# Row sums of the gates and the shift on VectorE, filler tiles at other places of the stream

## The chip, the cores and the metric

The kernel runs on one core of a Trainium2 chip. The metric is the device time of one execution in microseconds. Five engines work side by side, each through its own list of instructions in order: TensorE (PE in the profile; PEld is its weight load), VectorE (DVE), ScalarE (ACT), GpSimd (POOL) and SyncE (SP), which here only issues transfers. An instruction that waits holds up everything behind it on its engine.

## The reference

One step of a hybrid backbone with one layer: 128 context tokens and 512 latent tokens, 640 in all, of width 2048. Cut to what matters:

```
mod = silu(c) @ w_mod + b_mod            # for latent and for context: two vectors of 3 * 2048
shift, scale, gate = split(mod, 3)
h = rms_norm(x, norm_w) * (1 + scale) + shift
proj = h @ w_in                          # u_f, z_f (512 each), q, k, v, z_d (1536 each), a/b (48)
y_f = fft(u_f).real * silu(z_f)
q, k, v = silu(short_conv(q, k, v))      # q and k normalised
o = gated_delta_scan(q, k, v, a, b)      # 12 heads of 128, forward and backward
y = concat(y_f, rms_norm(o) * silu(z_d)) @ w_out
out = rms_norm(x + gate * y)
```

The gate needs `silu(c) @ w_mod[:, 4096:6144]` for two vectors; the shift's part in `u_f` needs `shift @ w_in[:, 0:512]`. Both are sums of 2048 weight rows, each row weighted by one number for each of the two vectors. These are the row sums of this case.

## The kernel before, in words

**Stages.** To about 200 us the kernel normalises the tokens, forms scale and shift and starts the projection. Then comes the stream: 53 tiles of 128 columns of `w_in` (`stream`, L1341), each 96 matmuls at L1354: 16 blocks of 128 rows, two halves of 320 tokens, three products of high and low parts of weight and token. ACT loads the weights (`raw`) and rounds them (`whi`, L1330), POOL subtracts (`wlo`, L1338). After the stream comes the output projection (L1622).

**Heads.** Between the stream's matmuls stand the short steps of the twelve heads, each a generator: `conv` (L731), `blocks` (L811), `solve` (L868), `decay` (L951), `prep` (L1002), `scan` (L1055), `head_out` (L1146). In `solve`, DVE builds small inverses, SP stores them to DRAM (`xd`) and loads them back in eight transfers, four `DD` (L912) and four `DP` (L915); DVE transposes `DD` (L918) and PE multiplies (L929, L940). A scan walks five blocks from both ends: PE gives keys and queries times state (L1072, L1079), DVE forms `r` (L1075), PE (L1091) and ACT (L1094) make `vn`, PE makes the update (L1099) from which DVE forms the new state `S` (L1106), and the output (L1111), which DVE adds (L1118, L1121). At its end come squares on ACT (L1137), a sum on DVE (L1139), a power on POOL (L1141) and a scaling on DVE (L1143); then `head_out` transposes the output on PE (L1154).

**Order.** All of it is recorded in one program order by a builder. `Estimate` (L72) keeps a clock for each engine with assumed costs. A generator yields the engine its next step needs and the time from which it may be recorded; `advance` (L1413) records every step that is due before the stream goes on. Ranks (L1656) decide between steps: scans and solves have low numbers, `res_gates` has 10, the last. The order that results is fixed; the real engines then wait wherever the assumed times were too short.

**Order of the tiles.** `names` (L1300) starts with u0 to u3, k1, q1, v1, z0, z1, f0, f1, f2; then each head h from 2 brings k, v, q and a filler, z of the head before (none for head 2; z10, f3, z11 for head 11). A tile k or q of head i may be handed over only when head i-2's scan is done, v only when the one before has been read (`needs`, L1480); until then the stream stalls.

**The row sums.** `rows256` (L1265) sums 256 columns: four loads of 512 KB into one buffer `gw`, after each four 32-wide matmuls that lie side by side in PE (L1273), and one addition into `ga` on DVE (L1276; L1278 the first time). It is called twice for the shift (`shift_u`, L1253) and eight times for the gates (`res_gates`, L1282). For the shift, PE then sums the four partition groups and turns them (L1260). For the gates it sums them (L1291), DVE adds the bias (L1292), which SP has loaded (L1288), and SP stores two rows (L1294). The Fourier steps wait for all gates to be done.

Of the kernel before, what the change touches and what calls it, by code (L numbers as in the profile page):

```python
# [9 lines left out]
F32 = mybir.dt.float32  # L10
F32R = mybir.dt.float32r
AF = mybir.ActivationFunctionType
ALU = mybir.AluOpType
# [4 lines left out]
P = 128  # L18
DM = 2048
NK = DM // P  # L20
# [51 lines left out]
class Estimate:  # L72
# [107 lines left out]
    def __call__(self, inst, *_):  # L180
        outs = [x.bass_ap for x in inst.outs if getattr(x, "bass_ap", None) is not None]
        ins = [x.bass_ap for x in inst.ins if getattr(x, "bass_ap", None) is not None]
        if not outs:
            return
        engine = str(inst.engine).split(".")[-1]
        if engine not in self.free:
            return
        op = str(inst.opcode)
        by = "DMA" if "DMA" in op else engine
        t = max([self.free[engine]] + [self.after(x, by, False) for x in ins] + [self.after(x, by, True) for x in outs])  # L190
        if by == "DMA":
            self.free[engine] = t + 0.06
            size = 4
            for _, count in outs[0].ap:
                size *= count
            piece = max(4, min(self.run(outs[0]), self.run(ins[0]), 8192))
            begin = max(t + 1.4, self.dma)
            self.dma = begin + size / piece * (7 + 0.043 * piece) / 16e3
            end = self.dma + 0.7
        else:  # L200
            end = t + self.cost(op, engine, inst, outs, ins)
            self.free[engine] = end
            if engine == "PE":
                end += 0.2
        for x in ins:
            self.note(x, end, by, False)
        for x in outs:
            self.note(x, end, by, True)
        self.last = max(self.last, end)
# [3 lines left out]
def hybrid_step(ctx: ExitStack, tc: tile.TileContext, x_prompt, x_sample, state_ctx, c, c_ctx,  # L213
# [3 lines left out]
    PE, ACT, DVE, POOL, SP = nc.tensor, nc.scalar, nc.vector, nc.gpsimd, nc.sync  # L217
    est = Estimate()
# [10 lines left out]
    def bank():  # L229
        return ps_g.tile([P, 512], F32, tag="g", name="bank")  # L230
# [6 lines left out]
    def K(name):  # L237
        a, b = CST[name]
        return cst[:, a:b]
# [4 lines left out]
    gates_d = dram.tile([2, DM], F32, name="gates_d")  # L244
# [23 lines left out]
    csh = const.tile([P, NK, 32], F32, name="csh")  # L268
# [282 lines left out]
    g = Pools()  # L551
# [316 lines left out]
    def solve(h):  # L868
# [42 lines left out]
        for b in range(4):  # L911
# [1 line left out]
                         in_=xd[10 * b:10 * b + 10].rearrange("u r c -> r u c"))  # L913
            o = 32 * (b ^ 1)
            SP.dma_start(out=DP[o:o + 32], in_=xd[10 * b + 5:10 * b + 10].rearrange("u r c -> r u c"))  # L915
        yield "V"
        f2, N = "p d t c -> p (d t c)", s["N"]
        DVE.transpose(DD[:, 2:4].rearrange(f2), DD[:, 0:2].rearrange(f2))  # L918
        yield
# [330 lines left out]
        yield  # L1250


    def shift_u():  # L1253
        while "ebias" not in done:
            yield "poll"
        for i in range(2):
            ga = yield from rows256(win_v[:, :, 256 * i:256 * i + 256], csh)
            pg = bank()
            for q in range(2):
                PE.matmul(pg[:, 2 * q:2 * q + 2], lhsT=ga[:, P * q:P * (q + 1)], rhs=K("sel_mod"), start=True, stop=True)  # L1260
            DVE.tensor_copy(ubias[:, 2 * i:2 * i + 2].rearrange("p i m -> p (i m)"), pg[:, 0:4])
            yield
        done.add("ubias")

    def rows256(src, lhs):  # L1265
        ga = g.tile([P, 256], F32, tag="ga", name="ga", bufs=1)
        for j in range(4):
            gw = g.tile([P, 4, 256], F32, tag="gw", name="gw", bufs=1)
            SP.dma_start(out=gw, in_=src[:, 4 * j:4 * j + 4])
            yield "P", est.last + 3.0  # L1270
            pg = bank()
            for q in range(4):
                PE.matmul(pg[32 * q:32 * q + 32, 0:256], lhsT=lhs[:, 4 * j + q, :], rhs=gw[:, q, :], start=True, stop=True,  # L1273
                          tile_position=(0, 32 * q))
            if j:
                DVE.tensor_tensor(ga, ga, pg[:, 0:256], ALU.add)  # L1276
            else:
                DVE.tensor_copy(ga, pg[:, 0:256])  # L1278
        yield
        return ga  # L1280

    def res_gates():  # L1282
        yield from shift_u()
        for i in range(8):
            ns = slice(2 * DM + 256 * i, 2 * DM + 256 * i + 256)
            ga = yield from rows256(wmv[:, :, ns], cz)
            bt = g.tile([P, 4, 256], F32, tag="gw", name="gbt", bufs=1)[0:2, 0]
            SP.dma_start(out=bt, in_=b_mod[0, ns].partition_broadcast(2))  # L1288
            yield "P", est.last + 1.0
            pg = bank()  # L1290
            PE.matmul(pg[0:2, 0:256], lhsT=K("sel_mod"), rhs=ga, start=True, stop=True)  # L1291
            DVE.tensor_tensor(bt, bt, pg[0:2, 0:256], ALU.add)  # L1292
            yield "S"
            SP.dma_start(out=gates_d[:, 256 * i:256 * i + 256], in_=bt)  # L1294
            yield
        done.add("res_gates")


    place = {"k": C_K, "v": C_V, "q": C_Q, "z": C_ZD, "u": 0, "f": 512}
    names = "u0 u1 u2 u3 k1 q1 v1 z0 z1 f0 f1 f2".split()  # L1300
    fill = {2: "", 11: "z10 f3 z11"}
    for h in range(2, NH):
        names += [f"k{h}", f"v{h}", f"q{h}"] + fill.get(h, f"z{h - 1}").split()
    tiles = [(n[0], int(n[1:]), place[n[0]] + P * int(n[1:])) for n in names]
# [396 lines left out]
```

## Time and profile before

| | us |
|---|---|
| median of three runs (lowest, highest) | 1458.52 (1456.28, 1462.25) |
| the profiled execution, own time | 1462.74 |
| its span in the trace | 1460.9 |
| PE busy, of the span | 1400.6 |
| DVE, ACT, POOL busy | 695.1, 670.8, 627.6 |

The span runs from the first to the last instruction of the profiled execution; what lies around it is 1.8 us. A row of a group of instructions gives its line, engine, operation, what it writes and reads, count, busy time, the mean of one, and the idle time of the engine just before it with what ended it. One PE instruction on 32-bit numbers leaves two records. The chain of waits is followed back from the last instruction; each of its rows is a start, a duration and a piece of work.

### The profile page before, as it was taken

To read this page: it belongs to the slowest core of one execution; us is meant where nothing else is said; L and a number is where in the kernel's file an instruction comes from. 1 tells how busy PE (TensorE), PEld (TensorE's weight loads), DVE (VectorE), ACT (ScalarE), POOL (GpSimd) and SP (SyncE) were. 2 spreads that over 40 slices of the span, in tenths; PEclk is the share of its full clock that TensorE was granted. 3 is DMA by queue.
4 is the path that set the end of the run, shared out by engine and by line. 5 is a ranking of instruction groups with operands and counts; after the bars stand their busy time and mean duration, and the time that the engine had idled before them with its cause. 6 is when DMAs were issued, how large, how long until landed. Compare 5 with 4: busy or idle time off the path is not lost.

```text
span 1460.9 us, 31546 instructions
## 1 busy us (share of the span) xinstructions
PE 1400.6 (96%) x12548; PEld 1272.2 (87%) x12548; DVE 695.1 (48%) x1476; ACT 670.8 (46%) x1808; POOL 627.6 (43%) x649
## 2 busy tenths in 40 slices
PE   6999989999999999999999999999999998999996
PEld 4799869878999889889999999899999996888885
DVE  5441115664346644746474646457463745322025
ACT  5332226634456445354555555455555454323134
POOL 2233213443334534344464544545364442337375
PEclk9999989999999999999999999999999999999998
DMA  9988973553454533433233333333242435494103
GB/s 304 271 264 267 309 202 105 151 147 102 140 146 123 141 124 95 144 106 90 83 91 87 86 107 83 106 87 106 72 112 62 137 111 178 148 323 163 44 1 144
DMA packets 268880, 203.21 MB, mean 139 GB/s; under 512 B 54649, under 2 KB 238918, under 8 KB 268606
## 3 DMA queue, kind: packets, MB, share of 16 engines
q1 hardware_dynamic: 146110, 129.36, 28.9%
q10 hardware_dynamic: 122624, 71.84, 17.1%
q8 instruction: 99, 1.62, 0.5%
q14 instruction: 47, 0.39, 0.1%
HBM read 177.16 MB, written 23.99 MB: 138 GB/s over the span
## 4 chain that ended last, share of the span: by engine, by line
PE 75%; DVE 9%; DMA 6%; ACT 2%; SPq 2%; issue 2%; POOL 1%; DVEq 0%; ACTq 0%; POOLq 0%
PE mbank L1354 40%; PE bank L1622 8%; PE mbank L1622 7%; PE bank L430 2%; DVE tmp L898 2%; PE bank L1091 1%; DMA DD<-xd 1%; PE bank L1111 1%; PE bank L1099 1%; PE bank L1072 1%; DVE tmp L885 1%; PE bank L1079 1%; PE bank L1273 1%; PE bank L587 1%; SPq L875 1%
## 5 line engine op out<-in xcount | busy, mean ns | idle before, releaser
L1338 POOL TENSOR_TENSOR wlo<-raw,whi 128x512 fp32r<-128x512 f32 x232 | 327.0, 1413 | 550.4 <-ACT whi L1330 463.0
L1354 PE MATMUL mbank<-h_hi,whi 128*128 128x320 f32 (+1 forms) x1696 | 556.0, 328 | 0.0
L1354 PE MATMUL mbank<-h_lo,whi 128*128 128x320 f32 (+1 forms) x1696 | 528.0, 311 | 0.0
L1354 PE MATMUL mbank<-h_hi,wlo 128*128 128x320 f32 (+1 forms) x1696 | 527.9, 311 | 0.0
L1354 PEld LDWEIGHTS mbank<-h_hi,whi 128*128 128x128 f32 x1696 | 321.9, 190 | 24.7 <-issue 20.3
L1354 PEld LDWEIGHTS mbank<-h_lo,whi 128*128 128x128 f32 x1696 | 322.3, 190 | 0.1
L1354 PEld LDWEIGHTS mbank<-h_hi,wlo 128*128 128x128 f32 x1696 | 321.9, 190 | 0.0
L1330 ACT CAST whi<-raw 128x512 fp32r<-128x512 f32 x232 | 142.2, 619 | 226.1 <-PE mbank L1354 155.3
L283 POOL TENSOR_TENSOR wlo<-raw,whi 128x512 fp32r<-128x512 f32 (+1 forms) x44 | 55.2, 1264 | 87.0 <-ACT whi L282 72.8
L1622 PE MATMUL mbank<-wlo,y_hi 128*128 128x512 f32 x160 | 63.7, 398 | 2.6 <-POOL wlo L283 2.0
L1622 PE MATMUL mbank<-whi,y_lo 128*128 128x512 f32 x160 | 64.1, 401 | 2.1 <-DVE y_lo L1509 2.0
L1622 PE MATMUL mbank<-whi,y_hi 128*128 128x512 f32 x160 | 64.1, 401 | 1.3 <-ACT y_hi L1507 1.3
L1094 ACT ACTIVATE vn<-bank,s 128x128 f32<-128x128 f32 x120 | 37.4, 364 | 57.1 <-PE bank L1091 56.7
L1622 PE MATMUL bank<-whi,y_hi 128*128 128x512 f32 x160 | 63.2, 395 | 0.0
L1622 PE MATMUL bank<-wlo,y_hi 128*128 128x512 f32 x160 | 63.1, 395 | 0.0
L1622 PE MATMUL bank<-whi,y_lo 128*128 128x512 f32 x160 | 63.1, 395 | 0.0
L1106 DVE SCALAR_TENSOR_TENSOR S<-S,egl,bank 128x128 f32<-128x128 f32 x72 | 21.8, 344 | 77.7 <-PE bank L1099 77.6
L282 ACT CAST whi<-raw 128x512 fp32r<-128x512 f32 (+1 forms) x44 | 24.6, 578 | 57.0 <-PE bank L1622 18.6
L885 DVE TENSOR_TENSOR tmp<-NP,XB 40x4 f32<-40x4 f32 (+6 forms) x84 | 31.1, 371 | 33.3 <-DMA NP<-pd 26.6
L1084 POOL TENSOR_SCALAR kd<-k,edl 128x128 f32<-128x128 f32 x96 | 45.4, 487 | 0.3
L977 ACT ACTIVATE E<-gb,ngg 128x128 f32<-128x128 f32 x120 | 40.2, 397 | 11.6 <-DVE AT L980 9.3
L829 POOL TENSOR_TENSOR nk<-sk,cst 128x5 f32<-128x5 f32 x12 | 14.1, 1179 | 63.2 <-DVE sk L826 56.3
(336 smaller groups left out, 2452.7 us busy)
## 6 DMA issues: line engine op xcount, KB each, us to landing
raw<-in_w_in ACTq DMA_DIRECT2D x106, 512.0 KB
wm<-in_w_mod SPq DMA_DIRECT2D x64, 512.0 KB
gw<-in_w_mod SPq DMA_DIRECT2D x32, 512.0 KB
raw<-in_w_out ACTq DMA_DIRECT2D x48, 256.0 KB
gb<-gd SPq DMA_DIRECT2D x12, 640.0 KB
yd<-zs SPq DMA_DIRECT2D x16, 320.0 KB
yt<-yd SPq DMA_DIRECT2D x16, 320.0 KB
out<-res SPq DMA_DIRECT2D x10, 512.0 KB
```

The source lines that it names most:

```text
L282: ACT.copy(whi, raw_part)
L283: sub.tensor_tensor(wlo, raw_part, whi, ALU.subtract)
L430: PE.matmul(acc_a[i][:, 0:384], lhsT=w, rhs=h[kt][:, 256:NT], start=kt + n == 0, stop=last)
L885: DVE.tensor_tensor(tv, NPd[:, :, i, 0:i].unsqueeze(2).broadcast_to(s4), Xd[:, :, 0:i, 0:i].rearrange("p h j c -> p h c j"), ALU.mult)
L898: DVE.tensor_tensor(tv, A.unsqueeze(2).broadcast_to(s4), B.rearrange("p j c -> p c j").unsqueeze(1).broadcast_to(s4), ALU.mult)
L977: ACT.activation(E[:, 1 - d], gb[:, d, P * t:P * (t + 1)], AF.Exp, bias=ngg4[:, d, h, t:t + 1])
L1084: POOL.tensor_scalar(kd[:, d], k[:, tt[d], :], edl4[:, d, h, tt[d]:tt[d] + 1], 1.0, ALU.mult, ALU.mult)
L1094: ACT.mul(vn[:, d], pv[:, P * d:P * (d + 1)], s["s3"][:, d, tt[d]:tt[d] + 1])
L1330: ACT.copy(his[c], raws[c // 2][:, 4 * (c % 2):4 * (c % 2) + 4])
L1338: POOL.tensor_tensor(lo, raws[c // 2][:, 4 * (c % 2):4 * (c % 2) + 4], his[c], ALU.subtract)
L1354: PE.matmul(pm[:, 0:b - a], lhsT=w, rhs=h[k][:, a:b], start=k + m == 0, stop=k == NK - 1 and m == 2)
L1622: PE.matmul(acc[t], lhsT=a[kk][:, sl], rhs=w, start=kk == order[0] and j == 0, stop=kk == order[-1] and j == 2)
```

## The change

`rows256` is written anew. It loads 16 blocks of rows in eight chunks of two (256 KB each) into one half of the tile `gw`; the other half holds the running sums for both vectors. For each block and vector DVE multiplies the rows with a weight for each partition and adds: one `tensor_scalar` for each first block and vector, `scalar_tensor_tensor` for the others, 32 instructions a call and 320 in all. Each partition then holds a partial sum, and PE adds the partitions with a matrix of ones: four one-column products a call for the shift, four 32-wide ones over 128 columns for the gates. The bias is loaded into 128 partitions in four transfers and the result stored in four. A chunk's DVE work may be recorded 1.0 us after the builder's assumed landing.

Two pacing numbers change: the builder counts 0.4 us for each issue of a transfer in place of 0.06, and the transpose L918 is held until 1.5 us after the assumed landing of `DD`. In the order of the tiles, f1 moves behind z2 of head 3 and f2 in front of z10 of head 11.

```diff
@@ class Estimate, __call__
-            self.free[engine] = t + 0.06
+            self.free[engine] = t + 0.4
@@ solve, ahead of the transpose of DD
-        yield "V"
+        yield "V", est.written(DD) + 1.5
@@
+    def rows256(src, by):
+        x = g.tile([P, 4, 256], F32, tag="gw", name="gw", bufs=1)
+        gw, acc = x[:, 0:2], x[:, 2:4]
+        for j in range(NK // 2):
+            SP.dma_start(out=gw, in_=src[:, 2 * j:2 * j + 2])
+            yield "V", est.last + 1.0
+            for q in range(2):
+                for m in range(2):
+                    one = by[:, 2 * j + q, m:m + 1]
+                    if j + q:
+                        DVE.scalar_tensor_tensor(acc[:, m], gw[:, q], one, acc[:, m], ALU.mult, ALU.add)
+                    else:
+                        DVE.tensor_scalar(acc[:, m], gw[:, q], one, None, ALU.mult)
+        yield
+        return x
@@ shift_u
-                PE.matmul(pg[:, 2 * q:2 * q + 2], lhsT=ga[:, P * q:P * (q + 1)], rhs=K("sel_mod"), start=True, stop=True)
+                for m in range(2):
+                    PE.matmul(pg[:, 2 * q + m:2 * q + m + 1], lhsT=x[:, 2 + m, P * q:P * (q + 1)], rhs=K("ones")[:, 0:1],
+                              start=True, stop=True)
@@ res_gates
-            PE.matmul(pg[0:2, 0:256], lhsT=K("sel_mod"), rhs=ga, start=True, stop=True)
-            DVE.tensor_tensor(bt, bt, pg[0:2, 0:256], ALU.add)
+            for b in range(4):
+                PE.matmul(pg[32 * b:32 * b + 32, 0:P], lhsT=K("ones")[:, 0:32], rhs=x[:, 2 + b // 2, P * (b % 2):P * (b % 2) + P],
+                          start=True, stop=True, tile_position=(0, 32 * b))
+            DVE.tensor_tensor(bt, bt, pg[:, 0:P], ALU.add)
@@ order of the tiles
-    names = "u0 u1 u2 u3 k1 q1 v1 z0 z1 f0 f1 f2".split()
-    fill = {2: "", 11: "z10 f3 z11"}
+    names = "u0 u1 u2 u3 k1 q1 v1 z0 z1 f0".split()
+    fill = {2: "", 3: "z2 f1", 11: "f2 z10 f3 z11"}
```

More of the change, by code (lines that the diff above doesn't have):

```diff
@@ L1256, in shift_u @@
         for i in range(2):
-            ga = yield from rows256(win_v[:, :, 256 * i:256 * i + 256], csh)
+            x = yield from rows256(win_v[:, :, 256 * i:256 * i + 256], csh)
             pg = bank()
             for q in range(2):
-                PE.matmul(pg[:, 2 * q:2 * q + 2], lhsT=ga[:, P * q:P * (q + 1)], rhs=K("sel_mod"), start=True, stop=True)
+                for m in range(2):
+                    PE.matmul(pg[:, 2 * q + m:2 * q + m + 1], lhsT=x[:, 2 + m, P * q:P * (q + 1)], rhs=K("ones")[:, 0:1],
+                              start=True, stop=True)
             DVE.tensor_copy(ubias[:, 2 * i:2 * i + 2].rearrange("p i m -> p (i m)"), pg[:, 0:4])
@@ L1263, in shift_u @@
         done.add("ubias")
[L1265 to L1280, printed above, removed]
     def res_gates():
@@ L1284, in res_gates @@
         for i in range(8):
[L1285 to L1288, printed above, removed]
+            n0 = 2 * DM + 256 * i
+            x = yield from rows256(wmv[:, :, n0:n0 + 256], cz)
+            bt = x[:, 0, 0:P]
+            for b in range(4):
+                SP.dma_start(out=bt[32 * b:32 * b + 32], in_=b_mod[0, n0 + P * (b % 2):n0 + P * (b % 2) + P].partition_broadcast(32))
             yield "P", est.last + 1.0
             pg = bank()
-            PE.matmul(pg[0:2, 0:256], lhsT=K("sel_mod"), rhs=ga, start=True, stop=True)
-            DVE.tensor_tensor(bt, bt, pg[0:2, 0:256], ALU.add)
+            for b in range(4):
+                PE.matmul(pg[32 * b:32 * b + 32, 0:P], lhsT=K("ones")[:, 0:32], rhs=x[:, 2 + b // 2, P * (b % 2):P * (b % 2) + P],
+                          start=True, stop=True, tile_position=(0, 32 * b))
+            DVE.tensor_tensor(bt, bt, pg[:, 0:P], ALU.add)
             yield "S"
-            SP.dma_start(out=gates_d[:, 256 * i:256 * i + 256], in_=bt)
+            for b in range(4):
+                SP.dma_start(out=gates_d[b // 2:b // 2 + 1, 256 * i + P * (b % 2):256 * i + P * (b % 2) + P], in_=bt[32 * b:32 * b + 1])
             yield
```

## The prediction

> **What bounds the kernel now.** First the page's opening lines, then the busy time of each engine by stage, then who TensorE (PE) waited for.
>
> ```profile
> span 1460.9 us, 31546 instructions
> PE 1400.6 (96%) x12548; PEld 1272.2 (87%) x12548; DVE 695.1 (48%) x1476; ACT 670.8 (46%) x1808; POOL 627.6 (43%) x649
> ```
>
> A busy PE alone proves little, because a matmul's record overlaps the next one. The stages say more (columns: stretch, its length, busy time of PE, PEld, DVE, ACT, POOL, granted clock, DMA share, GB/s):
>
> ```profile
> 200.00:700.00 500.00, 479.46 (x4825) 438.22 (x4824) 267.93 (x584) 246.49 (x694) 200.99 (x217) 0.98 0.44 126
> 700.00:1000.00 300.00, 297.29 (x2979) 289.63 (x2978) 169.91 (x354) 161.79 (x466) 151.12 (x159) 1.00 0.32 89
> ...
> 1200.00:1250.00 50.00, 44.95 (x227) 36.70 (x226) 25.37 (x76) 22.19 (x54) 12.22 (x9) 0.97 0.45 150
> ```
>
> From 200 to 700 us PE is idle 20.5 us of 500, from 700 to 1000 us 2.7 of 300. The stream of projection matmuls stands between the heads' short steps and fills their latencies, so in these stages a microsecond of PE work taken out is nearly a microsecond of span, as long as no wait opens. The waits that exist, longest first:
>
> ```profile
> PE bank L929 <- DVE DD L918: 8.9, 9, 3.3
> ...
> PE bank L1040 <- DVE TA L1028: 1.9, 1, 1.9
> ...
> PE bank L1072 <- DVE S L1106: 1.1, 1, 1.1
> ```
>
> The largest inside the stream is L929, the solve's first product, behind L918, nine times. DVE and POOL have room on average; the question is what 320 more DVE instructions do to the steps queued with them.
>
> **Row sums leave PE.** Before, each of the ten 256-column sums takes four groups of four 32-wide matmuls at L1273, 40 groups in all (320 records, 8 a group). One group between stream matmuls, from the timeline:
>
> ```profile
> 601.45 0.31 PE L1354 MATMUL mbank<-h_hi,wlo 128*128 128x320 f32 x1
> 601.68 0.64 PE L1273 MATMUL bank<-gw,cz 128*32 128x256 f32 x8
> 602.25 0.41 PE L1354 MATMUL mbank<-h_hi,whi 128*128 128x320 f32 x1
> 602.50 0.31 PE L1354 MATMUL mbank<-h_lo,whi 128*128 128x320 f32 x1
> 602.65 0.31 PE L1354 MATMUL mbank<-h_hi,wlo 128*128 128x320 f32 x1
> ```
>
> The stream starts one matmul every 0.15 us (602.50 to 602.65). From 601.45 to 602.50 there are two steps and one group, 1.05 us, so the group costs 1.05 - 0.30 = 0.75 us, change of kind included. 40 x 0.75 = 30.0 us. The eight closing products of the gates go too:
>
> ```profile
> 332.02 0.52 PE bank L1291 x2
> ```
>
> 8 x 0.52 = 4.2 us. New are eight groups of four 32-wide matmuls over 128 columns. No row shows that form: half the columns bound it at 0.37 us, the old group at 0.75; I take 0.55, nearer the middle because the change of kind does not halve, so 4.4 us. The eight one-column products of the shift replace four two-column ones; I book nothing. Net PE work: -30.0 - 4.2 + 4.4 = -29.8 us. PE idles 4% of the first stretch, and work removed just ahead of a wait buys nothing there: I take 96%, **-29 us** (bounds -22 to -31).
>
> **The sums on DVE.** 20 TENSOR_SCALAR and 300 SCALAR_TENSOR_TENSOR of 128x256 come, L1276 and L1278 go. The nearest rows are a 128x256 operation with both inputs in SBUF, an operation with one input in PSUM, and POOL's subtraction (ns min/median/max):
>
> ```profile
> L979 DVE TENSOR_TENSOR KK<-KK,E 128x256 f32<-128x256 f32 x60 | 33.4, 557 | 1.5 <-ACT E L977 1.4
> ...
> L1276 DVE TENSOR_TENSOR ga<-ga,bank 128x256 f32<-128x256 f32 x30 | 12.4, 414 | 24.3 <-PE bank L1273 24.1
> ...
> L1278 DVE COPY ga<-bank 128x256 f32<-128x256 f32 x10 | 4.2, 420 | 6.2 <-PE bank L1273 6.2
> ```
> ```profile
> L979 DVE TENSOR_TENSOR KK<-KK,E x60: 380/412/1521, 265.3 to 1160.2; 128x256 f32<-128x256 f32 x60
> ```
> ```profile
> L1106 DVE SCALAR_TENSOR_TENSOR S<-S,egl,bank x72: 329/343/349, 329.4 to 1204.6; 128x128 f32<-128x128 f32 x72
> ```
> ```profile
> L1338 POOL TENSOR_TENSOR wlo<-raw,whi x232: 1262/1289/2266, 96.0 to 1278.0; 128x512 fp32r<-128x512 f32 x116
> ```
>
> At 0.557 us each, 320 cost 178 us; less 12.4 + 4.2 that is +161 us on DVE. Between 200 and 1000 us DVE was busy 267.9 + 169.9 = 437.8 of 800 us, so it goes to about 599, 75%: not a bound, but its slack shrinks. The order shows what is queued with them, for DVE near head 3's L918 (gw holds two chunks of rows and their running sum; DD is the inverse that the solve builds). Before:
>
> ```order
> L1106 SCALAR_TENSOR_TENSOR S<-S,egl,bank 128x128 x2
> L1121 TENSOR_TENSOR o<-o,bank 128x128 x2
> L1276 TENSOR_TENSOR ga<-ga,bank 128x256
> L1075 SCALAR_TENSOR_TENSOR r<-bank,neg_eg,v 128x128 x2
> L918 STREAM_TRANSPOSE DD<-DD 128x320
> ```
>
> and after:
>
> ```order
> L1264 SCALAR_TENSOR_TENSOR gw<-gw,cz 128x256 x4
> L1106 SCALAR_TENSOR_TENSOR S<-S,egl,bank 128x128 x2
> L1118 SCALAR_TENSOR_TENSOR o<-bank,eg,o 128x128
> L1121 TENSOR_TENSOR o<-o,bank 128x128
> L1118 SCALAR_TENSOR_TENSOR o<-bank,eg,o 128x128
> L1121 TENSOR_TENSOR o<-o,bank 128x128
> L1075 SCALAR_TENSOR_TENSOR r<-bank,neg_eg,v 128x128 x2
> L918 STREAM_TRANSPOSE DD<-DD 128x320
> ```
>
> One short addition that waited for PE has become four sums, about 2.2 us, that wait for a transfer, with the scan's state update S and then r behind them, and PE's L1072 and L1091 behind those. How much of a DVE wait reaches PE? DVE's longest waits for transfers were
>
> ```profile
> L885 DVE TENSOR_TENSOR tmp<-NP,XB 40x4 f32<-40x4 f32 (+6 forms) x84 | 31.1, 371 | 33.3 <-DMA NP<-pd 26.6 <-DMA gbt<-in_b_mod 4.5
> ...
> L918 DVE STREAM_TRANSPOSE DD<-DD 128x320 f32<-128x320 f32 x12 | 6.1, 511 | 17.4 <-DMA DD<-xd 10.8 <-DMA DP<-xd 4.3 <-issue 2.3
> ```
>
> 26.6 + 10.8 + 4.3 = 41.7 us. PE waited 1.9 + 1.1 = 3.0 us on DVE at the two other lines above: 7%. If each of the 80 chunks makes DVE wait up to 1 us, 7% of 80 is 6 us; I take **+5 us** (bounds 0 to 20, a quarter passed on). SP gets 88 more issues, 80 half-size chunks among them, and the solve's transfers queue behind them; that is part of the same bound.
>
> **The two pacing numbers.** They make the builder place L918 and L929 later. What they aim at, in the chain of waits:
>
> ```profile
> 605.53 0.46 SPq L915
> 605.99 0.04 issue
> 606.03 1.84 DMA DD<-xd
> 607.87 0.02 issue
> 607.89 0.52 DVE DD L918
> 608.42 0.04 issue
> 608.46 0.89 PE bank L929 x53
> ```
>
> SP issues take up to 0.46 us each, eight in a row, while the builder counted 0.06; PE stood 3.3 us here, the longest of the nine waits, and afterwards ran at a reduced clock:
>
> ```profile
> 610.00:620.00 10.00, 10.00 (x132) 0.84 0.48 143
> ```
>
> 16% of 10 us is 1.6 us. Up to 8.9 + 1.6 = 10.5 us is to be had; I take **-6 us** (bounds 0 to -10.5).
>
> **The fillers.** In the diff only two tiles move, f1 and f2; z2 stands behind q3 as before, so no time is booked for a third. The tiles of heads 2 and 3 come two places sooner, those from k4 on one. k2's tile must not be handed over before head 0's scan is done. PE around head 0's output transposes (L1154), before:
>
> ```order
> L1354 MATMUL mbank_4221<-h_hi_409,whi_3812 128x322
> L1354 MATMUL mbank_4221<-h_lo_425,whi_3812 128x322
> L1354 MATMUL mbank_4221<-h_hi_409,wlo_3871 128x322
> L1154 MATMUL bank_4246<-cst_69,o_3652 128x128 x4
> L1154 MATMUL bank_4252<-cst_69,o_3652 128x128
> L1354 MATMUL mbank_4221<-h_hi_410,whi_3812 128x322
> ```
>
> and after:
>
> ```order
> L1072 MATMUL bank<-S,KT 128x128 x2
> L1079 MATMUL bank<-S,QT 128x128 x2
> L1091 MATMUL bank<-r,KK 128x128 x2
> L1111 MATMUL bank<-vn,AT 128x128 x2
> L994 MATMUL bank<-jq,cst 32x160 x4
> L1012 MATMUL bank<-DD,KK 32x32 x20
> L1025 MATMUL bank<-DD,YT 32x32 x20
> L1278 MATMUL bank<-cst,gw 128x1 x4
> L1040 MATMUL bank<-TA,KK 64x64 x10
> L1154 MATMUL bank<-cst,o 128x128 x5
> L1047 MATMUL bank<-KK,ET 64x64 x10
> ```
>
> The stream that stood around L1154 is gone from the last scan step: PE must sit through its latency once. From the last L1111 the outputs are added, squared, raised to a power and scaled:
>
> ```profile
> L1137 ACT ACTIVATE jk<-o 128x128 f32<-128x128 f32 x60 | 18.5, 309 | 13.5 <-DVE o L1121 10.4 <-POOL wlo L1338 1.8
> L1137 ACT ACTIVATION_READ_ACCUMULATOR jk<-o 128x1 f32 x60 | 11.2, 187 | 0.0
> ```
> ```profile
> L1141 POOL TENSOR_TENSOR m<-m,cst 128x5 f32<-128x5 f32 x12 | 19.4, 1619 | 24.9 <-DVE m L1139 24.5
> ```
> ```profile
> L1143 DVE TENSOR_TENSOR o<-o,m 128x640 f32<-128x640 f32 x12 | 12.2, 1017 | 5.2 <-POOL m L1141 5.2
> ```
>
> Four squares late at 0.309 + 0.187, one power, one scaling: 2.0 + 1.6 + 1.0 = 4.6 us, and some 2 us for two S, two r and two additions of about 0.343 each (L1106's duration). The small products L994 to L1040 stand in this gap of 6.6 us and cover part of it; which part is my choice, a third, so 4.4 us idle, and 1.6 us of reduced clock as after the stop above: **+6 us** (bounds 2 to 12, the latter if nothing is covered and a chunk of sums or two stand in the way). The Trainium skill (TensorE: Matmul & The Clock Gate, Part 1 on the clock gate) says that the clock halves only after about 3.4 us idle; the 3.3 us stop above agrees roughly, and a stall broken into shorter pieces would by that rule cost 4.4, not 6. At the stream's end the reverse holds: 5.1 us idle and 3% of 50 us lost clock between 1200 and 1250 us; with f2 there head 11 is further on when the stream ends, **-2 us** (bounds 0 to -6.5).
>
> **Sum.** -29 + 5 - 6 + 6 - 2 = -26 us. The profiled execution took 1462.74 us, 4.2 above the median of 1458.52; taken from the median, 1458.5 - 26 = 1432.5, so 1433 us.
>
> **Rivals.** *The stall is larger*: 12 us and a second half-clock window at the end of k2's tile, 8 more than booked: 1441 us. For it speaks the bare order, against it that PE's small products fill part. *The gain is given back*: the sums have one buffer, so each chunk waits for a transfer issued only after the previous four sums; if DVE waits 1.1 us a chunk (88 us) and 30% reaches PE, 26 us return: about 1458 us. Against it: 7% so far. *DVE becomes the bound* (slower): L979 goes to 1521 ns while L1106, with an input in PSUM, never leaves 329 to 349; POOL's subtraction takes 1289. So an operation with both inputs in SBUF at times sits out a POOL operation. The Trainium skill (SBUF — State Buffer, two separate sides) states this as an exclusive lock between such a DVE operation and GpSimd; the trace agrees. DVE has 800 - (437.8 - 16.6) = 379 us for 320 sums, so it decides from 1.18 us a sum. At 1.25 us the stretch overruns by 21 us: 1458.5 + 21 = 1480 us. Against it stands the mean of 0.557 at POOL's present load.
>
> **How the numbers follow.** Forecast 0.69, larger stall 0.12, given back 0.11, DVE-bound 0.08. A measurement of this kernel can tell 0.5%, 7.3 us, from no change. The first two lie below 1451.2 but for about 0.01: faster 0.80, same 0.12, slower 0.08. All terms at their good ends give -46 and at their bad ends about +10; both together are unlikely. From 1420 to 1454 I leave out the DVE-bound case, half of the given-back one and 0.05 at the low end.
>
> **What would show it.** Right: PE work 25 to 30 us less, the sums near 0.55 us each, L929's wait nearly gone, one stop of 3 to 8 us before head 0's L1154 near 310 us. Wrong: PE waiting for S, r or DD behind L1264 by over 15 us, or sums above 1 us.

## The result and the profile after

The changed kernel took 1441.28 us (median of four runs, 1437.84 to 1444.94) against 1457.40 us (1455.55 to 1462.25) before: 16 us less by the medians; the ratio is 0.9878 [0.9857, 0.9899]. The ratios given, here and below, differ by up to 0.12% from the quotient of the two medians, which here is 0.9890. Two executions far slower than all others (2657 us of e1, 1891 us of e4) are left out of all numbers. The profiled execution took 1442.66 us, 20.1 less than that of before. The opening lines of its page:

```profile
span 1440.9 us, 31437 instructions
PE 1373.0 (95%) x12284; PEld 1267.6 (88%) x12284; DVE 842.6 (58%) x1756; ACT 670.8 (47%) x1808; POOL 628.4 (44%) x649
```

DVE is busy 147.5 us longer, PE 27.6 us less, and PE's share of the span falls from 96 to 95%: PE stands still longer than before. The stages (columns as before: stretch, length, PE, PEld, DVE, ACT, POOL, granted clock, DMA share, GB/s):

```profile
200.00:700.00 500.00, 471.03 (x4791) 452.93 (x4788) 362.19 (x764) 263.92 (x747) 223.46 (x239) 0.97 0.40 112
700.00:1000.00 300.00, 293.97 (x3091) 284.43 (x3090) 227.38 (x464) 155.42 (x441) 141.73 (x148) 0.99 0.41 116
...
1200.00:1250.00 50.00, 49.98 (x236) 40.83 (x235) 21.48 (x32) 18.88 (x34) 17.07 (x14) 1.00 0.59 188
```

PE now idles 29.0 us of the first stretch (20.5 before) and 6.0 of the second (2.7), at a clock lower by 0.01 in each; between 1200 and 1250 us its 5.05 us of idle time and the 3% of lost clock are gone. Who PE waited for:

```profile
PE bank L929 <- DVE DD L918: 9.7, 7, 3.3
...
PE bank L1278 <- DVE gw L1264: 7.1, 2, 6.6
```

L929's wait has not gone. L1278, the shift's one-column products, is new in this list. The solve's lines keep their numbers; in the changed code the chunk is loaded at L1258, the sums stand at L1266 (the first) and L1264, and the stream's matmul is L1360.

**The sums themselves.** The row of the sums and the spread of their durations (ns min/median/max):

```profile
L1264 DVE SCALAR_TENSOR_TENSOR gw<-gw,cz 128x256 f32<-128x256 f32 x240 | 130.6, 602 | 5.6 <-DMA gw<-in_w_mod 5.4
```
```profile
L1264 DVE SCALAR_TENSOR_TENSOR gw<-gw,cz x240: 432/477/1566, 357.3 to 1026.1; 128x256 f32<-128x256 f32 x120
```

Most take 0.48 us and some 1.5, as L979's did; the mean is 0.602 here and 0.567 for the shift's, where 0.557 was taken. Of all 300 sums 34 took over 0.8 us, and each of these stood beside POOL operations for more than half of its time; of the 236 that took at most 0.52 us, 45 did. This fits the reading that a sum at times sits out a POOL operation. It brings the mean a quarter above the median, not to twice it: DVE is 362.2 + 227.4 = 589.6 us busy of the 800 between 200 and 1000 us, 74%. The wait for chunks is small too, 5.4 us here and 9.6 us before the shift's sums.

**A gate's new group on PE**, between stream matmuls:

```profile
436.18 0.31 PE L1360 MATMUL mbank<-h_hi,wlo 128*128 128x320 f32 x1
436.43 0.43 PE L1295 MATMUL bank<-gw,cst 128*32 128x128 f32 x8
436.78 0.41 PE L1360 MATMUL mbank<-h_hi,whi 128*128 128x320 f32 x1
437.03 0.31 PE L1360 MATMUL mbank<-h_lo,whi 128*128 128x320 f32 x1
```

From 436.18 to 437.03 are 0.85 us; less two steps of the stream, 0.55 us, the value taken.

**The longest new stop** stands at the shift. DVE around it, then PE, then the stretches:

```profile
255.92 1.67 DVE L1264 SCALAR_TENSOR_TENSOR gw<-gw,csh 128x256 f32<-128x256 f32 x4 [1.99 <-DMA gw<-in_w_in]
257.51 0.88 DVE L752 SCALAR_TENSOR_TENSOR vT<-pj,cw,vT 128x641 f32<-128x641 f32 x1
...
262.21 1.62 DVE L1264 SCALAR_TENSOR_TENSOR gw<-gw,csh 128x256 f32<-128x256 f32 x4
```
```profile
263.49 1.87 PE L1278 MATMUL bank<-cst,gw 128*128 128x1 f32 x8 [6.62 <-DVE gw L1264]
```
```profile
250.00:260.00 10.00, 6.87 (x47) 6.43 (x46) 6.61 (x13) 7.76 (x22) 3.52 (x6) 0.96 0.44 138
260.00:270.00 10.00, 6.51 (x30) 6.51 (x31) 7.67 (x17) 4.82 (x18) 3.11 (x3) 0.53 0.28 66
```

The sums of the last of the eight chunks come late. Those of the chunk before it, at 255.92, waited 2.0 us for their transfer, and from 257.51 to 262.21 4.7 us of a head's steps stood in DVE's list ahead of the last. (The last transfer was issued at 257.62 us, when the buffer was free, so a part of this time had to be waited anyway.) PE's list has the products at a fixed place, so PE stood 6.62 us. The clock was at one half for 10.2 us, from 259 us, 4.2 of them within the stop; in the rest, by stretches of half a microsecond, PE lost 3.0 us more: 9.6 us in all. Before the change, PE waited 1.0 us there (L1260 for `ga`) and the clock between 250 and 280 us was 1.00. The products themselves take 1.87 us a call, one of the eight records every 0.23 us, at that lower clock.

**The stop at k2's tile.** From the chain of waits, the stretch ahead of head 0's output transposes (start, duration, piece), and PE's stretches:

```profile
331.31 2.54 DVE gw L1264 x4
...
337.27 2.59 DVE gw L1264 x4
339.86 0.51 DVE S L1106 x2
...
343.74 2.40 DVE gw L1264 x4
...
349.36 1.20 DVE gw L1264 x3
...
350.60 1.86 PE bank L1278 x8
...
353.73 1.26 PE bank L1154 x5
```
```profile
340.00:350.00 10.00, 5.04 (x176) 3.99 (x176) 8.29 (x26) 3.42 (x15) 4.05 (x9) 0.90 0.27 87
350.00:360.00 10.00, 9.56 (x85) 8.84 (x78) 6.03 (x15) 4.08 (x11) 2.79 (x5) 0.59 0.24 81
```

Nearly four chunks of sums stand between the scan's own steps, 2.5 + 2.6 + 2.4 + 1.2 = 8.7 us of DVE. PE is idle 5.0 + 0.4 us and loses 4.2 us of clock while busy: 9.6 us. Before, PE was busy from 340 to 360 us throughout, at full clock. That the sums lie on this chain doesn't show that they make the stop; e2 and e11 below test it.

**An account of lost time.** For each program, from its profiled execution: stops (span less PE busy), half clock (in stretches of half a microsecond, PE's busy time times one less the granted clock, summed), and work (the span less both, PE's work at full clock). The last column sums the rows of PE's waits that name a DVE instruction. They are single executions. S stands for sums on DVE, P for both pacing numbers, F for the moved fillers.

| program | parts | ratio to before | stops | half clock | lost | work | PE waits on DVE |
|---|---|---|---|---|---|---|---|
| before | none | 1 | 60.3 | 16.0 | 76.3 | 1384.6 | 17.3 |
| e3_pacing_only | P | 0.9984 | 59.9 | 16.6 | 76.5 | 1385.5 | 19.3 |
| e2_fillers_only | F | 1.0062 | 72.2 | 17.9 | 90.1 | 1384.3 | 27.4 |
| e1_fillers_back | S P | 0.9943 | 79.6 | 19.9 | 99.5 | 1358.8 | 33.1 |
| e4_no_pacing | S F | 1.0047 | 85.3 | 31.3 | 116.6 | 1353.8 | 44.8 |
| after | S P F | 0.9878 | 67.9 | 18.3 | 86.2 | 1354.7 | 23.1 |
| e12_old_issue_cost | S F, half of P | 0.9950 | 76.6 | 26.6 | 103.2 | 1353.1 | 36.7 |
| e5_products_held | S P F | 0.9902 | 72.8 | 21.9 | 94.7 | 1356.4 | 25.4 |
| e11_sums_paused | S P F | 0.9919 | 70.5 | 14.0 | 84.5 | 1360.3 | 25.7 |
| e13_guard_after | S P F | 0.9919 | 69.3 | 25.8 | 95.1 | 1355.6 | 33.7 |
| e15_sums_in_pairs | S P F | 1.0047 | 86.5 | 28.2 | 114.7 | 1355.0 | 28.2 |
| e16_sums_dearer | S P F | 0.9920 | 68.1 | 19.7 | 87.8 | 1358.5 | 23.9 |
| e6_groups_twice | none | 1.0056 | 52.5 | 9.4 | 61.9 | 1400.7 | 18.9 |
| e14_guard_before | none | 0.9954 | 56.4 | 10.6 | 67.0 | 1384.6 | 12.9 |

From before to after the work falls by 29.9 us and the lost time rises by 9.9: 20.0 us of span. The medians differ by 16 us only, so with the same work the lost time rose by some 14.

Two stretches sort the programs, with idle time and half clock of PE added up. From 325 to 365 us, around k2's tile, the nine programs with moved fillers lose 8.0 to 16.2 us and the five with the old ones 0.1 to 0.8, with or without sums on DVE. From 250 to 290 us, around the shift's products, eight of the nine programs with sums on DVE lose 7.8 to 10.5 us (e16 1.1) and the five without 1.1 to 2.7.

### The profile page after: what moved, and what is told of

It is laid out like the page before. It is cut to its first block, busy times and chain, and to the rows that moved or that the text cites. A ratio compares the mean times of both kernels' runs of the same rounds, so it can differ in the third digit from the quotient of the medians.

```text
span 1440.9 us, 31437 instructions
## 1 busy us (share of the span) xinstructions
PE 1373.0 (95%) x12284; PEld 1267.6 (88%) x12284; DVE 842.6 (58%) x1756; ACT 670.8 (47%) x1808; POOL 628.4 (44%) x649
## 4 chain that ended last, share of the span: by engine, by line
PE 55%; DVE 17%; DMA 4%; ACT 2%; issue 2%; SPq 2%; POOL 1%; ACTq 0%; DVEq 0%; POOLq 0%
PE mbank L1360 28%; PE bank L1628 8%; PE mbank L1628 7%; DVE tmp L898 3%; DVE gw L1264 3%; DVE tmp L885 2%; PE bank L1091 1%; PE bank L1111 1%; PE bank L1099 1%; PE bank L1072 1%; DMA DD<-xd 1%; PE bank L1079 1%; DVE XB L887 1%; PE bank L841 1%; DVE YB L900 1%
## 5 line engine op out<-in xcount | busy, mean ns | idle before, releaser
L1360 PE MATMUL mbank<-h_hi,whi 128*128 128x320 f32 (+1 forms) x1696 | 554.3, 327 | 0.0
L1360 PE MATMUL mbank<-h_lo,whi 128*128 128x320 f32 (+1 forms) x1696 | 528.3, 311 | 0.0
L1360 PE MATMUL mbank<-h_hi,wlo 128*128 128x320 f32 (+1 forms) x1696 | 528.0, 311 | 0.1
L1360 PEld LDWEIGHTS mbank<-h_hi,whi 128*128 128x128 f32 x1696 | 322.5, 190 | 10.7 <-issue 7.4
L1360 PEld LDWEIGHTS mbank<-h_lo,whi 128*128 128x128 f32 x1696 | 322.7, 190 | 0.1
L1360 PEld LDWEIGHTS mbank<-h_hi,wlo 128*128 128x128 f32 x1696 | 322.2, 190 | 0.3 <-POOL wlo L1344 0.3
L1264 DVE SCALAR_TENSOR_TENSOR gw<-gw,cz 128x256 f32<-128x256 f32 x240 | 130.6, 602 | 5.6 <-DMA gw<-in_w_mod 5.4
L977 ACT ACTIVATE E<-gb,ngg 128x128 f32<-128x128 f32 x120 | 41.7, 396 | 32.6 <-DVE AT L980 25.4
L282 ACT CAST whi<-raw 128x512 fp32r<-128x512 f32 (+1 forms) x44 | 24.6, 579 | 56.4 <-PE bank L1628 19.1
L965 POOL TENSOR_TENSOR gb<-gb,cst 128x640 f32<-128x640 f32 x24 | 37.0, 1558 | 27.7 <-DMA gb<-gd 27.7
```

The costliest lines, as they stand in the source:

```text
L965: POOL.tensor_tensor(gv, gv, masks[d].unsqueeze(1).broadcast_to([P, 5, P]), ALU.add)
L977: ACT.activation(E[:, 1 - d], gb[:, d, P * t:P * (t + 1)], AF.Exp, bias=ngg4[:, d, h, t:t + 1])
L1264: DVE.scalar_tensor_tensor(acc[:, m], gw[:, q], one, acc[:, m], ALU.mult, ALU.add)
L1360: PE.matmul(pm[:, 0:b - a], lhsT=w, rhs=h[k][:, a:b], start=k + m == 0, stop=k == NK - 1 and m == 2)
```

## The experiments

The first theory after the result: PE's work fell as counted, and the rest went into two new stops of 10 us or so each, at the shift's products and at k2's tile, which can be cured one by one. The rivals: each part has no fixed value, or the fillers carry the gain. Each ratio below is to the kernel before on the same chip; the changed kernel was not timed again beside the variants, so a variant is compared with it by two ratios. Where not said otherwise, each edit is to the changed kernel.

**e1_fillers_back: the fillers at their old places.**

```diff
-    names = "u0 u1 u2 u3 k1 q1 v1 z0 z1 f0".split()
-    fill = {2: "", 3: "z2 f1", 11: "f2 z10 f3 z11"}
+    names = "u0 u1 u2 u3 k1 q1 v1 z0 z1 f0 f1 f2".split()
+    fill = {2: "", 11: "z10 f3 z11"}
```

> The changed kernel with f1 and f2 back in front of k2; row sums on VectorE and the pacing numbers stay. The theory (the sums take some 27 us of work from TensorE; two stops give back some 20 us of that, one before the shift's products L1278 of 6.6 us and one at the end of k2's tile of 5 us, each followed by about 10 us at half clock; the output stage starts better and gains 9 us) expects the stop at k2's tile to go and the better end to go with it: 1441 us, between 1436 and 1446. Rival, the moved fillers are a loss: 1432 us. Rival, the moved fillers carry the gain: 1450 us or more.

Measured: 1456.56 against 1463.89 us, 0.9943 [0.9921, 0.9965]. Without the move of the fillers half of the gain is gone. Where it went at the end of the stream, three kernels over the same stretch: before, after, and this one.

```profile
1180.00:1250.00 70.00, 64.95 (x376) 56.19 (x375) 33.60 (x114) 30.92 (x76) 17.19 (x18) 0.98 0.45 146
```
```profile
1180.00:1250.00 70.00, 69.98 (x367) 59.53 (x366) 35.36 (x79) 31.82 (x70) 22.40 (x18) 1.00 0.53 172
```
```profile
1180.00:1250.00 70.00, 59.74 (x325) 49.21 (x324) 35.12 (x100) 27.49 (x67) 15.54 (x17) 0.93 0.40 127
```

PE idles 5.1, 0.0 and 10.3 us there, and loses 1.7, 0.0 and 4.5 us of clock. That is 15 us in place of 6.8, and none in the changed kernel. The reading is that the last heads' latencies lie bare where no filler is left for them.

**e2_fillers_only: the kernel before, with only the fillers moved.**

```diff
-    names = "u0 u1 u2 u3 k1 q1 v1 z0 z1 f0 f1 f2".split()
-    fill = {2: "", 11: "z10 f3 z11"}
+    names = "u0 u1 u2 u3 k1 q1 v1 z0 z1 f0".split()
+    fill = {2: "", 3: "z2 f1", 11: "f2 z10 f3 z11"}
```

> The kernel before with only f1 and f2 moved. The theory expects a stop at the end of k2's tile and a better end that cancel: 1457 us, between 1451 and 1462. Rival, the fillers carry the gain: 1448 us or less. Rival, the fillers are a loss: 1463 us or more.

Measured: 1473.94 against 1463.89 us, 1.0062 [1.0038, 1.0087]. Alone the move costs 0.6%. Its stop at k2's tile:

```profile
340.00:350.00 10.00, 8.59 (x162) 6.97 (x160) 5.04 (x17) 4.49 (x14) 5.53 (x10) 1.00 0.39 107
350.00:360.00 10.00, 6.57 (x45) 5.51 (x45) 5.13 (x9) 5.11 (x16) 3.43 (x5) 0.53 0.26 87
```

1.4 + 3.4 us idle and 3.7 us of clock, 8.5 us: the stop belongs to the fillers and is there without any sum on DVE. PE's waits in it, from the timeline (the last figure is the idle time before):

```profile
347.88 1.15 PE L1040 MATMUL bank<-TA,KK 64*64 64x64 f32 x20 [0.94 <-DVE TA L1028]
...
352.12 1.33 PE L1047 MATMUL bank<-KK,ET 64*64 64x64 f32 x20 [2.50 <-ACT ET L1042]
354.76 1.33 PE L1154 MATMUL bank<-cst,o 128*128 128x128 f32 x5 [1.31 <-DVE o L1143]
```

By stretches of half a microsecond the clock is at one half for 10.2 us, though no single idle time is longer than 2.50 us and products stand between.

**e3_pacing_only: the kernel before, with only the two pacing numbers.**

```diff
-            self.free[engine] = t + 0.06
+            self.free[engine] = t + 0.4
...
-        yield "V"
+        yield "V", est.written(DD) + 1.5
```

> The kernel before with only the two pacing numbers (0.4 us an issue, transpose held to 1.5 us after the assumed landing). The theory, from the wait of L929 that is 9.7 us after and 8.9 us before, expects nothing: 1457 us, between 1453 and 1461. The rival, that the numbers do what the prediction booked, expects 1447 to 1452 us.

Measured: 1461.67 against 1463.89 us, 0.9984 [0.9964, 1.0004], no change that can be told. L929's wait goes from 8.9 us, nine times, only to 7.9 us, four times.

**e4_no_pacing: the two pacing numbers taken back.** The last diff, the other way round.

> The changed kernel with the old pacing numbers (0.06 us an issue, transpose not held). The theory expects 1441 us, between 1437 and 1446. The rival, that the numbers matter once VectorE is fuller and the bus of issues longer, expects 1448 us or more.

Measured: 1471.74 against 1463.89 us, 1.0047 [1.0028, 1.0066]. Numbers that do nothing alone are worth 1.7% here (from 0.9878 to 1.0047). The wait, PE's stretches at its longest place, and there SP's first and last load of the inverse and DVE's transpose:

```profile
PE bank L929 <- DVE DD L918: 26.1, 8, 7.0
```
```profile
580.00:590.00 10.00, 7.97 (x55) 7.70 (x54) 9.83 (x17) 2.52 (x6) 1.59 (x2) 1.00 0.22 64
590.00:600.00 10.00, 5.01 (x172) 4.74 (x172) 3.89 (x11) 2.53 (x7) 2.56 (x2) 0.66 0.59 152
```
```profile
587.51 0.31 SPq L912 DMA_DIRECT2D DD<-xd  x1
...
590.88 0.45 SPq L915 DMA_DIRECT2D DP<-xd  x1
```
```profile
594.43 0.51 DVE L918 STREAM_TRANSPOSE DD<-DD 128x320 f32<-128x320 f32 x1 [3.94 <-DMA DP<-xd]
```

PE stands 7.0 us behind one L918. The eight loads take SP from 587.51 to 591.33 us, where the builder with 0.06 counted half a microsecond, and DVE waits 3.9 us for the last of them. The old numbers were too short here as they were in the kernel before; there the wait was 8.9 us in all.

**e5_products_held: the shift's products recorded 10 us later**, so that PE has stream matmuls at the place of the longest stop.

```diff
+            yield "P", est.written(x[:, 2:4]) + 10.0
```

> The changed kernel with the shift's one-column products on TensorE recorded 10 us after the builder's assumed end of their sums. The stop of 6.6 us in front of them and the 10 us at half clock behind it should go: the theory of the stops expects 11 us less than the changed kernel, a ratio of about 0.980 to the kernel before (0.976 to 0.984). Rival, the stop only moves to the next step that needs VectorE there: 0.988, as the changed kernel.

Measured: 1450.25 against 1463.36 us, 0.9902 [0.9886, 0.9918]. L1278 is gone from PE's waits, and the time is no better. The stop itself is not gone. From 250 to 290 us PE still idles 6.0 us and loses 3.2 us of clock, 9.2 in place of 9.6, now in the stream: its longest idle time there is for `wlo` from POOL, which had waited 6.5 us for a step of DVE. POOL, then PE:

```profile
270.43 1.19 POOL L829 TENSOR_TENSOR nk<-sk,cst 128x5 f32<-128x5 f32 x1 [6.52 <-DVE sk L826]
...
272.99 0.63 PE L1361 MATMUL mbank<-h_hi,wlo 128*128 128x320 f32 x1 [2.87 <-POOL wlo L1345]
```

Another wait came in a stretch where PE of the changed kernel was busy throughout:

```profile
PE bank L775 <- DVE KT L761: 5.1, 1, 5.1
```
```profile
410.00:420.00 10.00, 4.94 (x35) 4.70 (x34) 9.16 (x10) 3.07 (x7) 5.34 (x4) 0.80 0.51 134
```

So the edit took away one wait and left the stop nearly as long, as the rival said, and the lost time went from 86.2 to 94.7. This was the first blow to the theory of stops that can be cured one by one.

**e6_groups_twice: the kernel before, with each group of L1273 done twice.**

```diff
-            for q in range(4):
+            for q in list(range(4)) * 2:
```

> The kernel before with every group of four 32-wide products of the row sums done twice into the same place. The second group stands behind the first, so it pays no change of kind. If a group is TensorE's work at full price, as the prediction counted, it adds 40 x 0.57 = 23 us (0.57 us is the group in the chain of waits; 0.75 with the change of kind would make 30): ratio 1.013 to 1.021. Rival, that such groups lie in time that TensorE would wait anyway: under 1.005.

Measured: 1471.34 against 1463.36 us, 1.0056 [1.0033, 1.0079], less than expected. Two groups between stream matmuls:

```profile
405.31 0.31 PE L1354 MATMUL mbank<-h_hi,wlo 128*128 128x322 f32 x1
405.55 1.07 PE L1273 MATMUL bank<-gw,cz 128*32 128x256 f32 x16
406.56 0.41 PE L1354 MATMUL mbank<-h_hi,whi 128*128 128x322 f32 x1
406.81 0.31 PE L1354 MATMUL mbank<-h_lo,whi 128*128 128x322 f32 x1
```

From 405.31 to 406.81 less two steps of 0.15 are 1.20 us for both: the second costs 1.20 - 0.75 = 0.45, so 0.3 of the first group's 0.75 us is change of kind, which a removal saves and a doubling doesn't add. 40 x 0.45 = 18 us, and the account's work is 16.1 us higher. The ratio says +8 us: the rest is lost time that fell (61.9 us in its profiled execution, 1464.4 us, the shortest of its runs, so that the account shows it at its best).

**e11_sums_paused: e5's edit, and no chunk while head 0's scan runs**, so that no sum stands in the stop at k2's tile.

```diff
+            while ("prep", 0) in done and ("delta", 0) not in done:
+                yield "poll"
             SP.dma_start(out=gw, in_=src[:, 2 * j:2 * j + 2])
...
+            yield "P", est.written(x[:, 2:4]) + 10.0
```

> As the run with the products held, and no chunk of sums is issued from the end of head 0's preparation to the end of its scan. The chain of waits of the changed kernel has three and a half chunks, 8.7 us, on its way through head 0's scan, where the stream stands still at k2's tile. The theory expects another 4 to 9 us less than with the products held alone: ratio about 0.975 (0.970 to 0.981). Rival, the latency of the scan itself sets this stop: no difference to the run with the products held.

Measured: 1451.39 against 1463.36 us, 0.9919 [0.9896, 0.9942]. Nothing is gained. No sum stands in DVE's list from 325 to 349 us, and the stop at k2's tile is there all the same, with the waits of e2:

```profile
338.51 1.15 PE L1040 MATMUL bank<-TA,KK 64*64 64x64 f32 x20 [0.94 <-DVE TA L1028]
342.89 1.33 PE L1047 MATMUL bank<-KK,ET 64*64 64x64 f32 x20 [3.23 <-ACT ET L1042]
345.53 1.33 PE L1154 MATMUL bank<-cst,o 128*128 128x128 f32 x5 [1.31 <-DVE o L1143]
```

They are 5.5 us, and 3.2 us of clock come to them: 8.6 us in place of 9.6. So the rival held: the latency of the head's own steps sets this stop, and the sums add about 1 us to it.

**e12_old_issue_cost: only the issue's assumed cost back at 0.06 us, the hold of L918 kept.**

```diff
-            self.free[engine] = t + 0.4
+            self.free[engine] = t + 0.06
```

> The changed kernel with only the builder's cost of an issue put back to 0.06 us; the transpose of DD stays held to 1.5 us after the assumed landing. Without both numbers the kernel was slower by 1.7%, with waits of L929 up to 7 us and half clock behind them. If the cost of an issue is what counts: ratio about 1.00 to 1.005 to the kernel before. If the hold of the transpose counts: 0.988.

Measured: 1455.01 against 1463.36 us, 0.9950 [0.9933, 0.9967], between the changed kernel and e4: by these ratios the issue cost is worth 0.7% and the hold 1.0%, though a new order alone moved the time by as much (e15 below). Its longest wait is again L929's, 19.1 us.

**e13_guard_after and e14_guard_before: the builder's `GUARD` (how long after the assumed time of its inputs a step of PE is recorded) at 0.6 us for 0.3**, in the changed kernel and in the kernel before: can a general margin do what the pacing numbers do?

```diff
-    GUARD, LEAD, SLACK, CHUNK = 0.3, 0.4, 0.9, 2
+    GUARD, LEAD, SLACK, CHUNK = 0.6, 0.4, 0.9, 2
```

> The changed kernel with the builder's guard, the time by which a step of TensorE is recorded after its inputs, at 0.6 us in place of 0.3. By the traces so far the span less TensorE's stops and its time at half clock is 1416 us with the sums on TensorE and 1384 us without, whatever the order; what differs is the stops. If these come from a VectorE that is later than the builder assumes, a larger guard cures them with the sums on VectorE: stops and half clock under 45 us in the trace (56 in the changed kernel), ratio 0.980 or less. Rival, the stops are one-off places (k2's tile, the shift's products) that a guard doesn't reach: 0.988 or more.

> The kernel before with the guard at 0.6 us. It has few stops behind VectorE, so the theory expects less than in the changed kernel: stops and half clock 35 to 50 us (45 before), ratio 0.993 to 1.003. If it gains as much as the changed kernel, the guard is a matter of its own and says nothing of the sums.

Measured: 1450.22 against 1463.17 us, 0.9919 [0.9899, 0.9939], and 1456.10 against 1463.17 us, 0.9954 [0.9937, 0.9972]. The 45 and 56 us of these expectations come from an earlier sum that is some 30 us below the table's lost time in both kernels; by the table it went from 86.2 to 95.1 us in the changed kernel and from 76.3 to 67.0 in the kernel before. The margin makes the kernel before faster by 0.5% and the changed one slower by 0.4%, the reverse of what the theory expected. In the latter, a wait for the scan's state stands now beside L929's, 2.8 us in the changed kernel:

```profile
PE bank L1072 <- DVE S L1106: 8.1, 5, 3.8
```

**e15_sums_in_pairs: the four sums of a chunk recorded as two pairs**, so that a short step can stand between.

```diff
             for q in range(2):
+                if q:
+                    yield "V"
```

> The changed kernel with each chunk's four sums recorded as two pairs, with other steps of VectorE free to go between. If four sums in a row are what makes S, r and the solve late: stops and half clock below 50 us, ratio 0.978 to 0.985. Rival, the total of VectorE's work counts: 0.988 or more.

Measured: 1468.82 against 1463.17 us, 1.0047 [1.0030, 1.0064]: a clear miss, 1.7% slower than the changed kernel. PE's waits on DVE are not much longer (28.2 us); those on ACT, POOL and transfers are, 19.1, 9.6 and 14.2 us against 10.5, 5.4 and 12.5. The longest apart from L929 (14.7 us) and the first load:

```profile
PE mbank L1362 <- POOL wlo L1346: 5.5, 2, 4.5
```

No single place explains it; why this order is so much worse stays open. It speaks against the four sums in a row as the simple cause of the lost time.

**e16_sums_dearer: the builder's cost of a DVE operation with two inputs in SBUF raised**, since the sums take longer than it assumes.

```diff
-                return 0.21 + many / 960 * (1.75 if outs[0].ap[0][1] == 40 else 1.0 if psum else 1.25)
+                return 0.21 + many / 960 * (1.75 if outs[0].ap[0][1] == 40 else 1.0 if psum else 1.75)
```

> The changed kernel with the builder's cost of a VectorE operation on two inputs in SBUF at 1.75 cycles an element in place of 1.25 (0.68 us in place of 0.54 for a sum; the trace has a median of 0.48, a mean of 0.60 and up to 1.57). If the builder's too short times are the cause: stops and half clock below 50 us, ratio 0.978 to 0.985. Rival, the means are near enough and single long sums, beside a GpSimd operation, do the harm: 0.988 or more.

Measured: 1450.79 against 1463.17 us, 0.9920 [0.9896, 0.9943]. L929's wait nearly goes, as the prediction wanted it of the pacing numbers, and so does the shift's stop (1.1 us from 250 to 290 us). The time turns up elsewhere, 16.2 us of it from 325 to 365 us:

```profile
PE bank L775 <- DVE KT L761: 7.6, 2, 4.3
...
PE bank L1154 <- DVE o L1143: 4.1, 3, 2.7
...
PE bank L929 <- DVE DD L918: 3.6, 1, 3.6
```

## Why the prediction was right or wrong

The sign held, and 1433 us was 8 below the measured 1441; by the medians -26 stands against -16, by the profiled executions, which the account uses, against -20. What was worked out row by row held, and what was argued from single waits did not.

**PE work off, -29.8: right.** The account gives -29.9 from before to after; over all programs the work is 1384 to 1386 us with the groups on PE (1401 with each done twice) and 1353 to 1360 with the sums on DVE, whatever the order. The new group measures 0.55 us as taken. The change of kind is about 0.3 us of the old group's 0.75.

**DVE sums, +5: the direction right, the size wrong.** DVE's own share was right (0.57 to 0.60 us a sum, 147.5 us more, 74% busy), and the wait for chunks stayed small, so neither the chunk wait of the second rival nor DVE as the bound came. But more reaches PE than the 5 us. Where the other parts are alike, the sums raise the lost time by 23.0 us (e3 to e1) and 26.5 (e2 to e4), beyond the bound of 20. Where the pacing numbers and the fillers come with them, it rises by 28.1 (e14 to e13) and by 9.9 only from before to after. Over the programs with the sums on DVE, the mean of PE's waits on DVE is 30.5 us against 19.2 without, and of the half clock 22.9 against 14.1: +11 and +9. The step that failed put a price on DVE waiting for a transfer, and none on steps of PE and POOL that wait because DVE's list is longer, nor on the clock that PE loses after a stop that grows. Its 7% was too low besides: it left out the 8.9 us that PE stood behind L918, whose own waits for transfers are in the 41.7 us. With them it is 29%, which of 80 us would be 23. That amount is near what came, but not the way, since DVE waited for chunks only 17 us in all.

Where the sums make PE wait is shown at the shift alone: the wait for L1264 in the changed kernel, and 7.8 to 10.5 us lost from 250 to 290 us in eight programs with the sums on DVE against 1.1 to 2.7 without. For the rest of the 23 to 28 us it is inferred from these means. No run parts DVE's longer list from its rival, that the groups taken off PE had filled its waits; for this, a kernel with the sums on DVE that also keeps the old groups on PE would be needed. e6 fits the rival: more of these groups came with less lost time. The prediction's own sign of being wrong, over 15 us of PE waiting for S, r or DD, wasn't reached in the changed kernel: these waits are 13.3 us.

Measured in the whole time, the sums alone bring almost nothing: 0.9984 to 0.9943 with pacing and old fillers, 1.0062 to 1.0047 with moved fillers and no pacing, 0.4% and 0.15% (about what their intervals can tell from nothing), of the 2% by which the work falls. The 26 us that the second rival named came back there, by another way than it said.

**One-column products, booked at nothing: wrong.** They take 3.7 us themselves (two calls of 1.87 at half clock; at full clock a call takes 0.95 us in e5, and the one that it replaces 0.50), and before the first PE stops 6.6 us, with 3.0 us of clock lost. No term held this, since a wait of PE for the last chunk of a call was never looked for.

**Pacing numbers, -6: wrong as argued, though they matter.** L929's wait, nearly gone by the forecast, is 9.7 us in place of 8.9, and alone the numbers do nothing (0.9984). They don't cure the old wait; they keep a new one from opening: without them it is 26.1 us, and the time 1.7% higher.

**Fillers at k2's tile, +6: 9.6 measured**, inside the bounds of 2 to 12 and near the end that was tied to chunks of sums in the way. As the first rival said, the time at low clock was longer than booked, but the stop cost 3.6 us more, not 8. That this rival's total, 1441 us, is the measured one is luck: other terms made up the rest. The mechanism was right: the stop comes with the fillers, 8.5 us in e2 without any sums on DVE and 8.6 in e11 with none in it, so chunks in the way are not why it is near the upper bound. Its place was not: head 0's L1154 stands at 353.7 us, not near 310. The longest single idle time in the changed kernel's stop, 3.4 us, was PE's wait for `YT` on ACT. The prediction weighed a rule of the Trainium skill (TensorE: Matmul & The Clock Gate, Part 1 on the clock gate), that the clock halves only after about 3.4 us idle, by which a stop in shorter pieces would lose none. e2 measured otherwise: idle times of 0.94, 2.50 and 1.31 us with small products between them went with 10.2 us at half clock.

**Stream end, -2: -6.8 measured** (5.1 us idle and 1.7 of clock), the good bound, and against what stands there with the sums and the old fillers (e1) it is 15 us. The move alone doesn't bring it: from 1170 to 1270 us e2 loses 7.8 us, as the kernel before does. With the sums and the move, six of eight programs lose 0 to 2.4 us there, e11 and e15 8.2 and 9.8. This is how a move that costs 0.6% alone gains 0.65% beside the sums (0.9943 to 0.9878).

**The sum.** The forecast's terms for waits and clock, +5 - 6 + 6 - 2, were +3 us; the account has +10, 7 more. The work fell by 30, one more than the 29 booked. So -26 became -26 + 7 - 1 = -20, the difference of the two profiled executions. The other 4 us to the medians' -16 are scatter between executions: the profiled one of before lies 5.3 us above its median, that of after 1.4.

**The later theory, too, fell in part.** It held that single stops can be cured one by one. e5, e11 and e16 each took away or shortened a wait, and the lost time stayed at 84 to 95 us; in e5 and e11 the two stops themselves cost within 2 us of what they had, behind other waits. Each edit records the whole order behind it anew. What the runs show is that the sums on DVE came with some 10 to 28 us more of stops and half clock in each of these four pairs of programs, and that the three parts belong together: 1.2% faster, where the fillers alone make it 0.6% slower, the pacing numbers alone change nothing, and the sums added to either one bring 0.15 to 0.4%. How much of the difference between two orders of the same work is cause and how much is where the steps happen to fall, e15's 28 us over the changed kernel above all, stays open. None of the variants beat the changed kernel by these ratios.

## What to carry to other kernels

Work taken from a saturated engine can be counted row by row, but it is gained only as far as the order still has something to put in front of the short steps. Here 30 us of PE's work went and 10 to 28 us came back as waits and half clock, so such a change needs its fillers and its pacing chosen anew with it, and is to be measured with them. Taking away the row that names a wait is not taking away the stop: look at the same stretch again afterwards. A sum of single waits doesn't price a recorded order; here orders of equal work differed by up to 32 us of lost time, and a forecast should carry a spread of that size. After a stop, look at the granted clock of the next window before the stop is priced: at the two long stops here the half clock cost 3 to 4 us beside 5 to 7 of waiting.

## What the runs showed of the hardware

The half clock comes in pieces of one length. By stretches of half a microsecond, every time at half clock before the last 10 us in the kernel before, the changed one, e4, e14 and e15 adds up to 3.4, 6.8, 10.2 or (once, near 206 us before) 13.7 us, whatever the stop was: 3.4 us after the 3.3 us stop behind L929 before, 10.2 us with the 6.6 us stop at the shift. The Trainium skill (TensorE: Matmul & The Clock Gate, Part 1) says that the clock is set by activity in windows of 3413 ns which run on freely; these sums agree.

So a stop isn't priced by its longest idle time. One of 2.35 us in the changed kernel, from 661.06 us in an otherwise busy stretch, cost no clock:

```profile
660.00:670.00 10.00, 7.65 (x205) 6.66 (x204) 6.00 (x13) 3.60 (x10) 5.50 (x10) 1.00 0.53 157
```

In e2, 2.50 us among shorter idle times and 64x64 products went with 10.2 us at half clock.

A one-column matmul of 32-bit numbers over 128 rows is not free on PE: at half clock one of its two records starts every 0.23 us, and the sixteen records of both calls take 3.7 us; in e5, at full clock, eight take 0.95 us. Not every matmul on 32-bit numbers leaves two records: the stream's, whose weights are rounded to another 32-bit type (`fp32r` in the rows), leave one each, 5088 in all. And a visit of four narrow matmuls among the stream's costs 0.75 us alone but 0.45 for a second one behind it.
